# One expert table split ahead of time, eight expert tiles summed per PSUM product, five score tiles handed over late

## The chip, the cores and the metric

The kernel runs on one core of a Trainium2 chip, as one program. The metric is the device time of one execution in microseconds, the median of three runs. The program is written with a tile framework: the code names tiles and operations, and a scheduler at build time decides in which order each engine's queue holds them. At run time every engine (PE, DVE, ACT, POOL, and SP, which only issues DMAs) works through its own queue strictly in order and stops at the first instruction whose inputs or buffers are not ready.

## The reference

One layer: a pair of bidirectional linear-attention mixers on 1024 tokens (with 256 context tokens), then an expert block. The change is about the expert block and what can be prepared for it.

```
def peer(h, wq, k1, k2, u, v):
    q = (tok @ wq).reshape(-1, 8, 2, 128)            # 8 retrieval heads
    s1, s2 = scores of both halves against k1, k2    # 128 keys each
    top 16 of s1, top 16 of s2, top 16 of their 256 sums
    expert = i1 * 128 + i2;  gate = softmax(top_s)   # 128 experts a token
    act = gelu(einsum("pd,ped->pe", xb, u[expert]))
    out = einsum("pe,ped->pd", gate * act, v[expert])
```

`u` and `v` are tables of 16,384 experts (128 tiles of 128) times 1024 columns in float32.

## The kernel before

**Precision.** Large products use float32 operands split into two float16 halves: `split` (L92 to L94) makes the high half on ACT (a scaled copy) and the low half on DVE (scale and subtract). `mm3` (L96 to L101) then does three matmuls for each 128-row step: high x high, high x low, low x high.

**Stages.** (1) `hg_proj`, `hg_scan`, `gla_proj`, `gla_scan`, the "heads", until about 1290 us: input projections, each from a weight slab that `slab` (L175) loads through three buffers `w32`, splits into three buffers `w16`, and feeds to `proj`; there are 65 such slabs. Beside them scans, gates and norms. (2) The merge gates and modulations, to 1500 us. (3) The merge and the output projection, to 1860 us. (4) "Prep", to 2858 us: choosing and routing of tokens (`choosing`, `route`), and one-hot products (`oh`, `pgm`, `gs`) that build `G_d`, the gate of every (token, expert) pair for five of the eight token blocks. (5) The dense stage, to the end.

**Two ways to the experts.** Three token blocks (`GB`) gather their experts' rows: 768 indirect DMAs in all (`row`, issued by POOL at L940), each 128 rows of 4 KB, used by one DVE operation at L919 (dot product with `u`) or L924 (`gacc`, sum with `v`). They have `AHEAD` buffers and run from prep to the end, dosed by `gathers` and `feed`. The other five blocks (`DB`) are done densely: for each of the 128 expert tiles, `u_turn` transposes the `u` tile on PE (`put`), ACT copies it out twice and POOL makes the low half (`uT`, L967); `u_act` multiplies it with the tokens (`ph`, 48 matmuls) and applies GELU (`ac`). `weigh` multiplies `ac` by the gates (`gt`, read from `G_d`) and splits it (`w`). `v_tile` loads the `v` tile (`vn`) and splits it (`v16`). `out_unit` multiplies four tiles' `w` and `v16` into PSUM (`pe`, 24 matmuls for a token block) and DVE adds that to `acc` (L1162).

**Early tiles.** 80 of the 128 tiles' `ac` (the list `early`) are made in prep, one for each `U_US` of the planner's time there, and kept in DRAM (`act_d`), from where the dense stage reads them (`acr`). The other 48 (`live`) are made in the dense stage. It walks through 32 groups of `GR` = 4 experts and, while it prepares a group, does the five `out_unit` of the group before.

**Work between the heads.** `presplit` makes split copies in DRAM of the branch, output and query weights: 40 units, dosed by `meanwhile`, which each projection calls, at `PRE` = 0.25 units a call of full width. Their stores are on ACT's queue (`st_`), the loads on SP's (`ld`).

## Time and profile before

| | us |
|---|---|
| median of three runs (4222.70 to 4229.41) | 4222.92 |
| the profiled execution | 4229.67 |
| its span, first to last instruction | 4228.0 |
| PE busy in it | 3884.8 (92%) |
| DVE busy | 2938.6 (70%) |
| ACT busy | 1430.1 (34%) |
| POOL busy | 1683.9 (40%) |

PE is busy in 92% of the span, but this is an average over stages with different limits; the stages have to be read one by one, with the granted clock of PE (1.00 is its 2.4 GHz level, 0.50 its 1.2 GHz level) and the share of time in which the 16 DMA engines are busy.

### The profile page before, as it was taken

What the parts mean: (1) busy time and instruction counts of PE and PEld (TensorE: products, weight loads), DVE (VectorE), ACT (ScalarE), POOL (GpSimd) and SP (SyncE); (2) the same over time, 40 slices, a digit from 0 to 9 for tenths busy, and PEclk for the clock granted to TensorE, in tenths of its full rate; (3) what the DMA queues carried; (4) which work ended last, traced back from release to release, by engine and by line L of the source; (5) the groups of instructions that cost most, each with busy time, mean ns of one, the idle gap of its engine ahead of it and who ended that gap; (6) DMA issues with size and microseconds to landing.
All of it is one profiled execution on the core that took longest, in us unless ns stands there. A gap on an engine that the chain in (4) does not pass through costs nothing.

```text
span 4228.0 us, 60334 instructions
## 1 busy us (share of the span) xinstructions
PE 3884.8 (92%) x23802; PEld 2350.2 (56%) x23802; DVE 2938.6 (70%) x5132; ACT 1430.1 (34%) x2194; POOL 1683.9 (40%) x1197
## 2 busy tenths in 40 slices
PE   6999999999999999988999989986899989999997
PEld 2665665656655444445776667763445544444453
DVE  5345446242556414379987799977989999889998
ACT  5344444243343202034543334552222222222222
POOL 2011111010011012127655567635766666666663
PEclk9999999999999999999999999987999999999998
DMA  5222122221223583227887778869989999989996
GB/s 189 78 73 85 56 73 79 74 87 46 87 64 115 162 282 107 99 97 242 295 307 249 254 242 298 305 228 319 329 318 336 321 323 325 316 311 325 328 315 232
DMA packets 435306, 884.64 MB, mean 209 GB/s; under 512 B 28511, under 2 KB 245066, under 8 KB 431438
## 3 DMA queue, kind: packets, MB, share of 16 engines
q0 software_dynamic: 110592, 402.70, 27.3%
q1 hardware_dynamic: 202676, 320.19, 22.6%
q10 hardware_dynamic: 121754, 157.89, 10.6%
q8 instruction: 186, 3.05, 0.3%
q14 instruction: 98, 0.80, 0.1%
HBM read 764.80 MB, written 115.88 MB: 208 GB/s over the span
## 4 chain that ended last, share of the span: by engine, by line
PE 47%; DVE 25%; DMA 11%; issue 8%; ACT 6%; POOL 4%; SPq 0%; ACTq 0%; DVEq 0%; POOLq 0%
PE ph L100 5%; DVE row_False L919 5%; PE pe L100 5%; DVE gacc L924 4%; PE pgm L1065 3%; PE pq L100 3%; PE pj_f0h L100 3%; PE pv_g L100 2%; PE pv_h L100 2%; DMA row_False<-in_peer_u_dram,idx 2%; PE pj_f1h L100 2%; PE pj_m L100 2%; DMA vn<-in_peer_v_dram 2%; DMA acr<-act_d 2%; PE pso L100 2%
## 5 line engine op out<-in xcount | busy, mean ns | idle before, releaser
L100 PE MATMUL pe<-v,w 128*128 128x512 f16 x3840 | 883.8, 392 | 138.7 <-DVE acc L1162 104.7
L100 PE MATMUL ph<-hb,uT 128*128 128x256 f16 (+1 forms) x6144 | 892.2, 303 | 14.6 <-POOL uT L967 10.4
L100 PEld LDWEIGHTS <-uT 128*128 128x128 f16 x6144 | 609.4, 99 | 242.5 <-POOL uT L967 13.1
L100 PEld LDWEIGHTS <-w 128*128 128x128 f16 x3840 | 384.0, 100 | 623.0 <-issue 166.4
L940 POOL DMA_INDIRECT row_False<-in_peer_u_dram,idx x384 | 548.9, 1429 | 274.6 <-DVE row_False L919 169.2
L940 POOL DMA_INDIRECT row_True<-in_peer_v_dram,idx x384 | 503.6, 1311 | 264.1 <-DVE gacc L924 173.1
L924 DVE SCALAR_TENSOR_TENSOR gacc<-row_True,dots,gacc 128x1024 f32<-128x1024 f32 x381 | 539.7, 1416 | 39.4 <-DMA row_True<-in_peer_v_dram,idx 35.8
L919 DVE SCALAR_TENSOR_TENSOR row_False<-row_False,h2n 128x1024 f32<-128x1024 f32 x384 | 496.2, 1326 | 67.1 <-DMA row_False<-in_peer_u_dram,idx 66.7
L967 POOL TENSOR_TENSOR uT<-uf,uT 128x512 f16<-128x512 f32 x256 | 380.8, 1499 | 284.0 <-ACT uf L966 282.6
L93 ACT ACTIVATE v<-vn 128x1024 f16<-128x1024 f32 x128 | 135.1, 1055 | 501.9 <-DMA vn<-in_peer_v_dram 386.7
L979 ACT ACTIVATE ac<-ph 128x256 f32<-128x256 f32 (+1 forms) x256 | 110.1, 438 | 371.8 <-PE ph L100 367.1
L1065 PE MATMUL pgm<-oh 128*128 128x128 f16 x1280 | 176.4, 295 | 53.2 <-ACT gs L1066 38.8
L1066 ACT ACTIVATE gs<-pgm 128x512 f32<-128x512 f32 x160 | 171.0, 1069 | 136.6 <-PE pgm L1065 136.6
L94 DVE SCALAR_TENSOR_TENSOR v<-vn,v 128x1024 f16<-128x1024 f32 x128 | 168.2, 1314 | 50.5 <-ACT v L93 50.3
L1162 DVE TENSOR_TENSOR acc<-pe,acc 128x1024 f32<-128x1024 f32 x155 | 188.6, 1217 | 11.8 <-PE pe L100 11.7
L100 PE MATMUL pj_m<-hb,w_m 128*128 128x512 f16 x768 | 187.4, 401 | 2.3 <-DVE lf_g L86 1.6
L1065 PEld LDWEIGHTS <-oh 128*128 128x128 f16 x1280 | 145.7, 117 | 77.0 <-issue 63.5
L100 PE MATMUL pq<-hb,w_wq 128*128 128x512 f16 x768 | 180.0, 387 | 1.0 <-POOL hb L89 0.8
L964 ACT ACTIVATE uT<-put 128x512 f16<-128x512 f32 x256 | 155.0, 605 | 71.0 <-PE put L961 69.4
L89 DVE TENSOR_TENSOR oh<-iota,rTr 128x1024 f16<-128x1024 f16 x160 | 139.1, 879 | 33.9 <-PE pgm L1065 33.8
L100 PEld LDWEIGHTS <-hb 128*128 128x128 f16 x1536 | 150.2, 98 | 17.8 <-issue 0.3
L966 ACT ACTIVATE uf<-put 128x512 f32<-128x512 f32 x256 | 154.4, 603 | 8.9 <-POOL uT L967 8.8
(364 smaller groups left out, 5531.9 us busy)
## 6 DMA issues: line engine op xcount, KB each, us to landing
un<-in_peer_u_dram SPq DMA_DIRECT2D x128, 512.0 KB
vn<-in_peer_v_dram SPq DMA_DIRECT2D x128, 512.0 KB
G_d<-gs ACTq DMA_DIRECT2D x20, 2048.0 KB
gt<-G_d ACTq DMA_DIRECT2D x32, 1280.0 KB
act_d<-ac ACTq DMA_DIRECT2D x80, 320.0 KB
acr<-act_d SPq DMA_DIRECT2D x80, 320.0 KB
mw<-in_ada_w_dram SPq DMA_DIRECT2D x32, 512.0 KB
w_wq<-wq_d SPq DMA_DIRECT2D x32, 512.0 KB
```

The lines of the kernel that those rows point to most:

```text
L89: eng.tensor_tensor(out=out, in0=in0, in1=in1, op=op)
L94: return V.scalar_tensor_tensor(out=lo, in0=src, scalar=float(scale), in1=hi, op0=ALU.mult, op1=ALU.subtract)
L100: PE.matmul(ps, lhsT=a(k), rhs=b(k), start=n == 0, stop=n == last)
L919: V.scalar_tensor_tensor(out=row, in0=row, scalar=1.0, in1=h2n, op0=ALU.mult, op1=ALU.mult, accum_out=dots[:, s:s + 1])
L924: V.scalar_tensor_tensor(out=gacc[n], in0=row, scalar=dots[:, s:s + 1], in1=gacc[n], op0=ALU.mult, op1=ALU.add)
L940: G.indirect_dma_start(out=row, out_offset=None, in_=src[0], in_offset=bass.IndirectOffsetOnAxis(ap=gsel[n][0][:, s:s + 1], axis=0))
L964: S.activation(hi, pv, AF.Copy, scale=SU)
L966: S.activation(uf, pv, AF.Copy, scale=SU)
L967: pace[0] = G.tensor_tensor(out=lo, in0=uf, in1=hi, op=ALU.subtract)
L1065: PE.matmul(pgm[:, t, :], lhsT=oh[:, 0, :, t], rhs=oh[:, j, :, t], start=j == 2, stop=j == 3)
L1066: S.activation(gs[:, :, t0:t0 + TB].rearrange("p i n -> p n i"), pgm, AF.Copy, scale=SA / SG)
L1162: vmark[0] = V.tensor_tensor(out=acc[n], in0=ps, in1=acc[n], op=ALU.add)
```

## The change

Four things. `presplit` also splits all 128 tiles of the table `v` between the projections of the heads and keeps them as float16 pairs in DRAM (`v_d`); `v_tile` then only loads the pair. With that `PRE` is 0.95, its 168 units replace 40, and its stores move from ACT's queue to SP's. Groups have eight experts instead of four, so that an `out_unit` is 48 matmuls into PSUM and one addition; the gates are still read for four (`GH`); `w` and `v16` have 12 buffers each (8 before), and the five units of a group stand in the first half of the next. Score tiles are paced at `U_US` = 7.2 in prep; those that are left then (`rest`, five of them, read off the order of the changed program) are done at the start of the dense stage and stored there, in group 0. The set of early tiles is the first five of each eight instead of a spread. The gathered rows have 5 buffers instead of 6, `feed` has other weights, and the SBUF area reserved for descriptors of DMAs that POOL issues is set to 4096 bytes a partition.

```diff
-GR = 4
+GR = 8
+GH = 4
+NBUF = 12
-U_US = 6.2
+U_US = 7.2
-AHEAD = 6
-PRE = 0.25
+AHEAD = 5
+PRE = 0.95
-    early = [e for e in range(NKEY) if e * 5 % 8 < 5]
+    early = [e for e in range(NKEY) if e % 8 < 5]
...
+            def rows(src, dst, sc, nm):
+                w32 = wi.tile([P, D], F32, name=f"w32_{nm}", tag="w32", bufs=3)
+                ld(out=w32, in_=src)
+                w16 = ws.tile([P, 2, D], F16, name=f"w16_{nm}", tag="w16", bufs=3)
+                split(w32, w16[:, 0], w16[:, 1], sc)
+                ld(out=dst, in_=w16)
...
+            more = slabs()
+            for e in range(NKEY):
+                rows(v_r[e], v_d[e], SV, f"v{e}")
                 yield
+                if e % 3 == 2:
+                    next(more, None)
+                    yield
+            yield from more
...
-        while pend is not None:
-            early_tile()
...
-        tt(V, v3, v3, gt4[:, :, e % GR, :], ALU.mult)
-        w16 = pd.tile([P, 2, TD], F16, name=f"w16_{e}", tag="w16", bufs=2 * GR)
+        tt(V, v3, v3, gt4[:, :, e % GH, :], ALU.mult)
+        w16 = pd.tile([P, 2, TD], F16, name=f"w16_{e}", tag="w16", bufs=NBUF)
...
-        vn = pd.tile([P, D], F32, name=f"vn{e}", tag="vn", bufs=2)
-        ld(out=vn, in_=v_r[e])
-        v16 = pd.tile([P, 2, D], F16, name=f"v16_{e}", tag="v16", bufs=2 * GR)
-        vmark[0] = split(vn, v16[:, 0], v16[:, 1], SV)
+        v16 = pd.tile([P, 2, D], F16, name=f"v16_{e}", tag="v16", bufs=NBUF)
+        ld(out=v16, in_=v_d[e])
...
+    rest = [pend, *es] if pend is not None else []
+    todo = []
+    for j in range(GR):
+        todo += [j] * (j in live) + rest[2 * j:2 * j + 2]
+    todo += rest[2 * GR:] + [e for e in live if e >= GR]
...
-    work = lambda e: 2.1 if e in early else 9.5
+    work = lambda e: (7.5, 7.5, 7.5, 7.5, 1.0, 2.5, 2.5, 2.5)[e % GR]
...
+                if g == 0:
+                    for r in rest[2 * j:2 * j + 2] if j < GR - 1 else rest[2 * j:]:
+                        st_(out=act_d[early.index(r)], in_=next_act(r))
...
-                    for n in DB[j * NU // GR:(j + 1) * NU // GR]:
+                    for n in DB[min(j * NU // GH, NU):(j + 1) * NU // GH]:
                         out_unit(g - 1, n, *prev)
...
-    nc = _bacc.Bacc("TRN2", target_bir_lowering=False, num_devices=1)
+    nc = _bacc.Bacc("TRN2", target_bir_lowering=False, num_devices=1, dynamic_dma_scratch_size=4096)
```

**In the heads** SP's queue holds the loads of the weight slabs (`w_f1h`, `w_qh`, `w_gh`: slabs of a head's projections; `w_pb`: a branch weight for `presplit`). Before, between the slabs `w_f1h` and `w_qh`:

```order
L179 DMA w_f0h_999<-in_w_in_dram 128x8x128
L179 DMA w_f1h_1083<-in_w_in_dram 128x8x128
L179 DMA w_pb_1140<-in_w_branch_hgrn_dram 128x8x128
L179 DMA w_qh_1173<-in_w_in_dram 128x8x128
L179 DMA w_gh_1335<-in_w_in_dram 128x8x128
```

In the changed program, at the same two slabs (`w_v` is a tile of the table `v`, `v_d` and `br_d` are where split copies go):

```order
L182 DMA w_f1h_1144<-in_w_in_dram 128x8x128
L326 DMA br_d<-w_pb_1107 128x2048
L318 DMA w_v_1175<-in_peer_v_dram 128x1024
L321 DMA v_d<-w_v_1139 128x2048
L318 DMA w_v_1207<-in_peer_v_dram 128x1024
L182 DMA w_pb_1239<-in_w_branch_hgrn_dram 128x8x128
L321 DMA v_d<-w_v_1177 128x2048
L182 DMA w_qh_1246<-in_w_in_dram 128x8x128
```

One transfer stood between the two slabs, now six do, three of them stores that wait for a split.

**At the hand-over** from prep to the dense stage ACT's queue holds the last copies of the one-hot products (`gs`), the store of `G_d` and the reads of the gates (`gt`). Before:

```order
L1066 ACTIVATE gs_3_24807<-pgm_124_24902 128x4x128
L1068 DMA G_d<-gs_3_24807 128x4096
L1180 DMA gt_24949<-G_d 128x20x128
L93 ACTIVATE v_0_24955<-vn_24953 128x1024
L93 ACTIVATE v_1_25041<-vn_25039 128x1024
L1180 DMA gt_25193<-G_d 128x20x128
L1140 CAST w_0_24959<-acr_24951 128x640
```

In the changed program:

```order
L1082 ACTIVATE gs_3_24998<-pgm_124_25264 128x4x128
L980 ACTIVATE uT_25308<-put_1_25318 128x512
L1084 DMA G_d<-gs_3_24998 128x4096
L982 ACTIVATE uf_1_25324<-put_1_25318 128x512
L995 ACTIVATE ac_25327<-ph_120_25328 128x256
L995 ACTIVATE ac_25327<-ph_120_25354 128x384
L980 ACTIVATE uT_25383<-put_0_25384 128x512
L1223 DMA act_d<-ac_25327 128x640
L1212 DMA gt_25290<-G_d 128x20x128
```

Score tiles (`put`, `ph`; here tiles 120 and 121) now stand between the store of `G_d` and the reads of it, and four more follow.

**In the dense stage** DVE's queue holds the additions to `acc` (the number behind `pe` is the token block), the gathered rows' operations, the splits of `v` and of `w`. Before, over four additions:

```order
L1162 TENSOR_TENSOR acc_24926<-pe_6_28448,acc_24926 128x1024
L94 SCALAR_TENSOR_TENSOR v_44_28515<-vn_28513,v_44_28515 128x1024
L1162 TENSOR_TENSOR acc_24927<-pe_7_28474,acc_24927 128x1024
L924 SCALAR_TENSOR_TENSOR gacc_14435<-row_48_True,dots_24271,gacc_14435 128x1024
L1141 TENSOR_TENSOR w_44_28519<-acr_28511,w_44_28519 128x640
L924 SCALAR_TENSOR_TENSOR gacc_14435<-row_49_True,dots_24271,gacc_14435 128x1024
L94 SCALAR_TENSOR_TENSOR v_45_28555<-vn_28553,v_45_28555 128x1024
L924 SCALAR_TENSOR_TENSOR gacc_14435<-row_50_True,dots_24271,gacc_14435 128x1024
L1162 TENSOR_TENSOR acc_24923<-pe_2_28525,acc_24923 128x1024
```

In the changed program, from one addition to the next but one:

```order
L1174 TENSOR_TENSOR acc_25286<-pe_3_31206,acc_25286 128x1024
L935 SCALAR_TENSOR_TENSOR row_34_False,dots_30546<-row_34_False,h2n_30544 128x1024
L935 SCALAR_TENSOR_TENSOR row_35_False,dots_30546<-row_35_False,h2n_30544 128x1024
L935 SCALAR_TENSOR_TENSOR row_36_False,dots_30546<-row_36_False,h2n_30544 128x1024
L935 SCALAR_TENSOR_TENSOR row_37_False,dots_30546<-row_37_False,h2n_30544 128x1024
L935 SCALAR_TENSOR_TENSOR row_38_False,dots_30546<-row_38_False,h2n_30544 128x1024
L935 SCALAR_TENSOR_TENSOR row_39_False,dots_30546<-row_39_False,h2n_30544 128x1024
L91 TENSOR_TENSOR acr_31469<-acr_31469,gt_31467 128x640
L1174 TENSOR_TENSOR acc_25287<-pe_5_31282,acc_25287 128x1024
```

The splits of `v` are gone from DVE, and six or seven rows' operations stand between two additions where one to six stood.

## Rows read from the trace of the kernel before

**Rows 1.** The page: busy time of each engine.
```profile
PE 3884.8 (92%) x23802; PEld 2350.2 (56%) x23802; DVE 2938.6 (70%) x5132; ACT 1430.1 (34%) x2194; POOL 1683.9 (40%) x1197
```
**Rows 2.** Stages: window, length, busy PE, PEld, DVE, ACT, POOL, clock, DMA share, GB/s.
```profile
80.00:1290.00 1210.00, 1177.13 (x8071) 750.22 (x8069) 562.58 (x940) 475.97 (x664) 161.55 (x87) 0.99 0.24 72
1290.00:1500.00 210.00, 192.68 (x1060) 100.88 (x1058) 106.88 (x163) 48.10 (x74) 12.38 (x6) 0.95 0.54 170
1860.00:2858.00 998.00, 913.29 (x6518) 680.21 (x6516) 869.94 (x1976) 449.46 (x733) 587.66 (x444) 0.97 0.74 261
2878.00:4170.00 1292.00, 1178.03 (x6238) 623.76 (x6239) 1173.71 (x1289) 338.13 (x525) 842.57 (x585) 0.95 0.92 321
```
**Rows 3.** Timeline of PE in the dense stage: start, length, what; idle before, releaser.
```profile
3312.39 13.24 PE L100 MATMUL pe<-v,w 128*128 128x512 f16 x48 [4.89 <-DVE acc L1162]
3325.47 1.04 PE L961 MATMUL put<-ident,un 128*128 128x128 f32 x8
3326.35 6.68 PE L100 MATMUL ph<-hb,uT 128*128 128x256 f16 x48
3332.87 20.93 PE L100 MATMUL pe<-v,w 128*128 128x512 f16 x96
...
3394.63 5.75 PE L100 MATMUL pe<-v,w 128*128 128x512 f16 x14 [5.32 <-DVE acc L1162]
```
**Rows 4.** Groups by line, 2878 to 4170 us: busy, mean ns, idle before, releasers.
```profile
L100 PE MATMUL pe<-v,w 128*128 128x512 f16 x3686 | 847.4, 391 | 132.3 <-DVE acc L1162 98.3 <-ACT w L1140 27.7 <-DVE w L1141 5.5
...
L924 DVE SCALAR_TENSOR_TENSOR gacc<-row_True,dots,gacc 128x1024 f32<-128x1024 f32 x243 | 334.7, 1377 | 4.3 <-DMA row_True<-in_peer_v_dram,idx 1.7
L919 DVE SCALAR_TENSOR_TENSOR row_False<-row_False,h2n 128x1024 f32<-128x1024 f32 x253 | 319.5, 1300 | 22.5 <-DMA row_False<-in_peer_u_dram,idx 22.2
L1162 DVE TENSOR_TENSOR acc<-pe,acc 128x1024 f32<-128x1024 f32 x148 | 180.1, 1217 | 10.4 <-PE pe L100 10.3
L94 DVE SCALAR_TENSOR_TENSOR v<-vn,v 128x1024 f16<-128x1024 f32 x127 | 167.0, 1315 | 30.1 <-ACT v L93 30.0
...
L940 POOL DMA_INDIRECT row_True<-in_peer_v_dram,idx x250 | 334.1, 1336 | 212.7 <-DVE gacc L924 165.8 <-issue 27.7 <-DVE row_False L919 9.6
```
**Rows 5.** Two windows of 42 us in the dense stage, columns as in rows 2.
```profile
3554.00:3596.00 42.00, 34.22 (x171) 17.27 (x171) 38.22 (x52) 10.79 (x16) 27.11 (x20) 0.92 1.00 351
3596.00:3638.00 42.00, 42.00 (x239) 23.45 (x238) 33.23 (x44) 11.11 (x19) 25.68 (x17) 1.00 0.81 274
```
**Rows 6.** Who waited for the stores to wq_d: us, times.
```profile
  ACT w_m L93: 23.7, 5
  ACT w_gg L93: 8.4, 3
```
**Rows 7.** Groups by line, 1860 to 2858 us, PE.
```profile
L100 PE MATMUL ph<-hb,uT 128*128 128x256 f16 (+1 forms) x3936 | 582.9, 304 | 13.7 <-POOL uT L967 10.4 <-ACT ac L979 3.2
...
L961 PE MATMUL put<-ident,un 128*128 128x128 f32 x680 | 93.4, 277 | 6.2 <-ACT uf L966 6.2
```
**Rows 8.** Timeline of PE at the hand-over, 2824 to 2890 us.
```profile
2831.84 1.10 PE L1065 MATMUL pgm<-oh 128*128 128x128 f16 x8 [1.14 <-ACT gs L1066]
2877.97 1.46 PE L100 MATMUL pe<-v,w 128*128 128x512 f16 x3 [20.40 <-ACT w L1140]
```
**Rows 9.** The page's DMA parts: a queue's packets and MB; sizes of transfers.
```profile
q0 software_dynamic: 110592, 402.70, 27.3%
...
vn<-in_peer_v_dram SPq DMA_DIRECT2D x128, 512.0 KB
...
gt<-G_d ACTq DMA_DIRECT2D x32, 1280.0 KB
```
**Rows 10.** Timeline of PE, 4100 to 4228 us: its last product.
```profile
4199.66 13.34 PE L100 MATMUL pe<-v,w 128*128 128x512 f16 x48 [5.30 <-DVE acc L1162]
```
**Rows 11.** The chain that ended last, pieces in order of time: start, us, what.
```profile
2909.12 8.17 DMA row_False<-in_peer_u_dram,idx
...
3582.45 7.14 DMA row_False<-in_peer_u_dram,idx
```

More of the change, by code (lines that the diff above doesn't have):

```diff
@@ L130, in tile_layer @@
     wo_d = dram.tile([KC, P, 2, D], F16, name="wo_d")
+    v_d = dram.tile([NKEY, P, 2, D], F16, name="v_d")
     u_r = peer_u[0].rearrange("(e p) d -> e p d", p=NKEY)
@@ L311, in presplit, with slabs @@
         def presplit():
-            for j in range(KC):
-                for bi, w in ((0, w_br_gla), (1, w_br_hg)):
-                    st_(out=br_d[bi * KC + j], in_=slab(w[0], j * P, f"pb{bi}{j}", SW))
-                    yield
-            for k in range(KC):
-                w32 = wi.tile([P, D], F32, name=f"wo32_{k}", tag="w32", bufs=3)
-                ld(out=w32, in_=w_out[k * P:(k + 1) * P, :])
-                w16 = ws.tile([P, 2, D], F16, name=f"wo16_{k}", tag="w16", bufs=3)
-                split(w32, w16[:, 0], w16[:, 1], SW)
-                st_(out=wo_d[k], in_=w16)
+            def rows(src, dst, sc, nm):
[4 more added lines that the diff above has]
+                ld(out=dst, in_=w16)
+            def slabs():
+                for j in range(KC):
+                    for bi, w in ((0, w_br_gla), (1, w_br_hg)):
+                        ld(out=br_d[bi * KC + j], in_=slab(w[0], j * P, f"pb{bi}{j}", SW))
+                        yield
+                for k in range(KC):
+                    rows(w_out[k * P:(k + 1) * P, :], wo_d[k], SW, f"wo{k}")
+                    yield
+                for j in range(16):
+                    ld(out=wq_d[j], in_=slab(peer_wq[0], j * P, f"pq{j}", SWQ))
+                    yield
+            more = slabs()
+            for e in range(NKEY):
+                rows(v_r[e], v_d[e], SV, f"v{e}")
                 yield
-            for j in range(16):
-                st_(out=wq_d[j], in_=slab(peer_wq[0], j * P, f"pq{j}", SWQ))
-                yield
+                if e % 3 == 2:
+                    next(more, None)
+                    yield
+            yield from more
         ahead = presplit()
@@ L1166, in tile_layer, with next_act @@
     live = [e for e in range(NKEY) if e not in early]
-    uT = u_turn(live[0], u_load(live[0]))
-    li = 0
-    work = lambda e: 2.1 if e in early else 9.5
+    rest = [pend, *es] if pend is not None else []
[3 more added lines that the diff above has]
+    todo += rest[2 * GR:] + [e for e in live if e >= GR]
+    if not rest:
+        uT = u_turn(todo[0], u_load(todo[0]))
+    ahead_ = iter(todo[1:])
+    def next_act(e):
+        nonlocal uT
+        en = next(ahead_, None)
+        uTn = u_turn(en, u_load(en)) if en is not None else None
+        ac = u_act(e, uT)
+        uT = uTn
+        return ac
+    work = lambda e: (7.5, 7.5, 7.5, 7.5, 1.0, 2.5, 2.5, 2.5)[e % GR]
     left = [sum(map(work, range(NKEY))), 256 * len(GB) - done[0]]
@@ L1178, in tile_layer @@
         if g < NG:
-            gt4 = pd.tile([P, TD // NB, GR, NB], F32, name=f"gt{g}", tag="gt4", bufs=2)
-            st_(out=gt4, in_=G_d[:, :, g * GR:(g + 1) * GR, :].rearrange("b i j n -> i b j n"))
             cur = ([None] * GR, [None] * GR)
@@ L1183, in tile_layer @@
                 e = g * GR + j
+                if j % GH == 0:
+                    gt4 = pd.tile([P, TD // NB, GH, NB], F32, name=f"gt{e}", tag="gt4", bufs=2)
+                    st_(out=gt4, in_=G_d[:, :, e:e + GH, :].rearrange("b i j n -> i b j n"))
                 if e in early:
@@ L1187, in tile_layer @@
                 else:
[L1188 to L1193 removed]
+                    ac = next_act(e)
                 cur[1][j] = v_tile(e)
@@ L1210, in tile_layer @@
             for n in range(NT):
-                x1s[n] = pd.tile([P, D], F32, name=f"x1_{n}", tag="v16", bufs=2 * GR)
+                x1s[n] = pd.tile([P, D], F32, name=f"x1_{n}", tag="v16", bufs=NBUF)
                 ld(out=x1s[n], in_=x1_d[n * P:(n + 1) * P, :])
```

6 lines of the change are left out of this document (removed).

## The prediction

> **What bounds the kernel now.** I read the engines' shares first, then the table by stage, and in each stage the idle time in front of PE and what ended it. PE is busy for 3884.8 of 4228.0 us [rows 1], but the 343 idle us lie in few places. The heads (80 to 1290) are PE's: 1177.1 of 1210 us, only 32.9 idle, while DVE is busy for 562.6, ACT for 476.0 and the DMA engines for 0.24 of the stretch [rows 2]. So there is room beside PE for other work, as long as nothing makes PE's next weights late. Prep (1860 to 2858) has PE at 913 and DVE at 870 of 998 [rows 2]. Then PE stands for 20.4 us [rows 8]. The dense stage is the one to look at: PE 1178.0, DVE 1173.7 of 1292 us and the DMA share 0.92 at 321 GB/s. Three resources are above 0.9 there, so taking one away shows the next.
>
> Of the three, DVE is the one that PE waits for. Eight experts take 3394.63 - 3312.39 = 82.2 us, and at the start of each such piece PE stands for about 5 us with `acc` as releaser [rows 3]; over the stage `acc` released 98.3 of the 132.3 idle us in front of the `pe` products [rows 4]. `acc` is short (1.22 us), but stands in DVE's queue behind row operations and splits. After the stall 48 `pe` matmuls take 13.24 us, where 96 together take 20.93, that is 10.46 for 48 [rows 3], and the granted clock of such a window is 0.92 against 1.00 without the stall [rows 5]: the stall costs some 3 us more than itself. With no stall and full clock, eight experts are 240 `pe` x 0.218 (20.93/96) = 52.3, three live tiles at 0.88 + 6.52 = 7.40 from start to start [rows 3], 22.2: **74.5 us**.
>
> **The heads.** Each of the 128 tiles of `v` adds a load, an ACT copy, a DVE split and a store. The split costs 1.315 us of DVE [rows 4], 128 x 1.315 = 168 us, and ACT's copy no more than that; 562.6 + 168 and 476 + 168 stay far below 1210. The DMAs are 512 KB in and 512 KB out, 134 MB, which is 111 GB/s over 1210 us on top of 72; the stage at 1860 has moved 261 [rows 2]. The dose of 0.95 units a call ends the 170 units by the end of the merge gates (the calls of full width there and before are some 180); that stage stands at 170 GB/s [rows 2], so the same rate on top leaves it at 281, under the dense stage's 321. In total this is free. What is not free is order: the added units share SP's queue and the three buffers `w32` and `w16` with the weight slabs, and a store on SP waits for its split while the next slab's load is queued behind it. Of slab, split and store at work beside the heads the trace has 40 units. All of PE's idle time there is 32.9 us, 0.82 a unit, and that includes causes of their own; so 128 units cost from 0 to 128 x 0.82 = 105 us. I take **+25**, a quarter: part of what went before was that the stores sat in ACT's queue (23.7 us in 5 waits, 4.7 each, 8.4 in 3 [rows 6]) and ACT made the very splits that PE waited for; these waits go. An added unit also lacks room in no total.
>
> **Prep and hand-over.** 80 early tiles become 75 there, a difference of about 4.75 with the one that is in work at the end. One costs 582.9/82 = 7.11 for its `ph` and 93.4/85 = 1.10 for its `put` (3936 and 680 instructions, 48 and 8 a tile [rows 7]), 8.2 us; 4.75 x 8.2 = **-39**. The one-hot products (`pgm`) that end prep have no early tile left beside them now: the row shown is 1.1 us of work behind 1.1 us of idle time, and there are some 13 like it up to 2858, 15 us [rows 8]. With the slower pace tiles last to the end, **-15**. The gap of 20.4 us at the hand-over, in which `G_d` is stored and read back [rows 8], does not become shorter, but tiles 120 and 121 stand in it: its gain is in the next sum, since they would otherwise lie in front.
>
> **The dense stage.** From DVE go 128 splits of `v` (167.0 us) and half of the additions (180.1/2 = 90) [rows 4]; by the 15.7 pieces of eight experts in 1292 us, 16.4 of 74.7 us. DVE has 58 to 65 us of work per 74.5 and PE's wait for `acc` loses its cause: six or seven rows between two additions are at most 7 x 1.38 = 9.6 us, under the 10.5 of a unit's 48 matmuls. ACT loses the copies too. PE would fall to 74.5.
>
> Then DMA is next. In one piece of eight experts the changed kernel moves 32.5 rows of 402.70/768 = 0.524 MB [rows 9], 17.0; `v`, the same 512 KB a tile in halves, 4.2; three `un` 1.6; five `acr` of 128 x 640 x 4 bytes 1.6; two `gt` of 1280 KB 2.6: **27.1 MB**. The densest window has share 1.00 and 351 GB/s, and its neighbour 0.81 at 274 [rows 5], both 338 to 351 per unit of share. At 351 the 27.1 MB take 77.1 us, at 321, the mean of the stage before, 84.3. Both are over 74.5, so the transfers bind, by little. I take 345, **78.5 us**, nearer to the full window, as PE and DVE no longer stop at a fixed place. The Trainium skill, in "HBM Reference", section "Specifications (TRN2)", says that a core streaming alone measures about 425 GB/s; by that figure the piece would take an estimated 63.7 us and DMA would bind nothing. No row here shows more than 351, at a share of 1.00, so the sum goes by the row.
>
> Before, 2858 to the end was 1370 us. After: group 0 has three live tiles and five `rest` tiles, 8 x 7.4 = 59, no units, and the hand-over in it, whose first gates are needed 20 us in; from 55 (all hidden) to 83 (a whole piece, 59 + 20 and more), I take 75. Fifteen groups at 78.5 are 1177.5 (74.5 to 84.3 each). Then five last units, 52.3, and 15 from the end of PE's last product (4199.66 + 13.34 [rows 10]) to 4228, as now. Sum 1319.8, that is **-50**.
>
> Smaller edits. `acr` of the rest tiles is written and read back as before. The area for descriptors is 4096 bytes and no row shows how much is used; POOL issues a row in 1336 ns and has 27.7 us of idle time without a releaser in 250 issues [rows 4], so from the rows its cost is between 0 and what one row less in flight would cost, which is the second rival. I take 0.
>
> **Sum.** 4228 + 25 - 39 - 15 - 50 = 4149 on the profiled span. The median of the runs is 4222.9, 5.1 below that span (the profiled execution was at 4229.7, 6.8 above the median): **4144**.
>
> **The rivals.** *DMA does not bind.* If the share can stay at 1.00 with more than 351 GB/s, or the row queue's transfers merely stretch into idle room, PE is the limit: 74.5 a group, 55 for group 0. That is 15 x 4.0 + 20 = 80 less, **4064**. For it: PE and the engines are still stopped in every piece now, so nobody has seen the DMAs pushed. Against: the full windows occur already [rows 5]. The Trainium skill's section named above leads to this rival.
>
> *Five rows in flight are too few.* Rows are issued when a buffer comes free: five in issue (1.34 us), landing and use (1.35). In the 52 us of five units 26 rows stand in DVE's queue in front of the additions, one per 2.01 us. Five buffers keep up if landing takes at most 5 x 2.01 - 1.4 - 1.35 = 7.3 us. The chain has two row transfers of 7.14 and 8.17 us [rows 11], on both sides of that. At 8.17 a row comes every 2.18 us, 26 of them take 56.8, 4.5 more than the units: PE waits for `acc` again, by 15 x 4.5 = 67 us, **4211**. For it: waits for rows are 22.2 and 1.7 us with six buffers [rows 4], and a fuller DMA lands later.
>
> *The heads pay (the slower side).* The place is SP's queue in the heads, where between two slabs now stand six transfers, three of them stores which wait for a split, in a ring of three buffers. If the load of a slab is held until the store before it is released and PE is through its own work by then, each of the 65 slabs costs its lateness. In the trace a store held ACT for 4.7 us in the longer waits [rows 6]; the row of eight waits gives 4.0 in the mean, and `slab` has a lead of several us. Total gain elsewhere is 104, so it decides from 104/65 = 1.6 us a slab. At 2.8, the middle of 1.6 and 4.0, it is 182 instead of 25, **4301**. For it: PE has only 33 us of slack there. Against: PE's part of a slab is 1177/65 = 18 us, long against six transfers of 0.5 to 1 MB.
>
> **How the numbers follow.** Forecast 4144 with 0.50, DMA not binding 4064 with 0.20, five rows too few 4211 with 0.15, the heads' loss 4301 with 0.12, anything else 0.03. The measurement can tell about 0.2% from no change, so faster is below 4214.5 and slower above 4231.4. Faster: the forecast nearly whole, the first rival, and two thirds of the second, 0.79; same 0.07 (the rest of the second, and of the forecast if heads come to 105); slower 0.14. The range leaves out the slower rival and the far ends: 4055 (10 below the first rival, for heads at 15 instead of 25) to 4215 (the second).
>
> **What would show it.** Heads: PE idle between 80 and 1290 about 58 us instead of 33, the stage ending 25 later; if it grows by over 130 the third rival holds, and the trace must then name weights (`w_...`) as releaser of PE. Hand-over: `ph` products between the last `pgm` and the first `pe`. Dense: no 5 us stalls for `acc` at the head of a piece, clock 1.00, a period of 78.5 us for eight experts at a DMA share of 0.97 or more and about 345 GB/s, with PE's waits moved to `v`, `acr` or `uT` data that a DMA releases. If the period is 74.5 at a higher rate, the first rival; if DVE waits long for rows and PE for `acc` with the share below 0.95, the second. Wrong altogether would be a landing time of `row` transfers over 9 us.

## The result and the profile after

The changed kernel takes 4273.72 us (median; 4267.74 to 4277.66) against 4223.81 for the kernel before: a ratio of 1.0114, 95% interval 1.0097 to 1.0132. It is slower by 1.1%; 4144 was forecast, and the range ended at 4215. The profiled execution has a span of 4265.9 us, 37.9 more than before.

The table by stage of the changed kernel (window, length, busy PE, PEld, DVE, ACT, POOL, clock, DMA share, GB/s), to be read beside [rows 2]:

```profile
80.00:1290.00 1210.00, 1139.90 (x7634) 720.72 (x7633) 672.96 (x969) 560.84 (x741) 161.72 (x85) 0.97 0.50 163
...
1860.00:2858.00 998.00, 910.47 (x6354) 666.73 (x6352) 882.80 (x2135) 445.50 (x721) 552.27 (x425) 0.97 0.71 250
...
2878.00:4170.00 1292.00, 1173.85 (x6243) 626.55 (x6241) 973.78 (x1088) 225.93 (x415) 782.54 (x600) 0.95 0.92 328
```

In the heads PE loses 37 us of busy time and its granted clock falls from 0.99 to 0.97. In the dense stage DVE has 200 us less to do (257 were forecast), and PE is no busier for it: 1173.9 of 1292 us, where it was 1178.0. So the relief of DVE did not reach PE.

Four marks on PE's timeline cut the span: the first query product (`pq`), the last one-hot product (`pgm`, its start and length), and the first `pe` of the second and of the last group of eight. In the changed kernel:

```profile
1687.93 0.38 PE L102 MATMUL pq<-hb,w_wq 128*128 128x512 f16 x1
...
2858.50 1.10 PE L1081 MATMUL pgm<-oh 128*128 128x128 f16 x8
...
3048.92 4.70 PE L102 MATMUL pe<-v,w 128*128 128x512 f16 x21
...
4202.56 4.70 PE L102 MATMUL pe<-v,w 128*128 128x512 f16 x21
```

In the kernel before (whose groups have four experts; the last two marks have as many `pe` matmuls, 240, ahead of and behind them as in the changed kernel):

```profile
1621.88 0.38 PE L100 MATMUL pq<-hb,w_wq 128*128 128x512 f16 x1
...
2856.47 1.10 PE L1065 MATMUL pgm<-oh 128*128 128x128 f16 x8 [1.11 <-ACT gs L1066]
...
2976.25 4.04 PE L100 MATMUL pe<-v,w 128*128 128x512 f16 x10 [2.11 <-DVE acc L1162]
...
4142.73 3.57 PE L100 MATMUL pe<-v,w 128*128 128x512 f16 x8 [9.11 <-DVE acc L1162]
```

| | before | after | difference | forecast |
|---|---|---|---|---|
| to the first `pq` (heads, merge) | 1621.9 | 1687.9 | +66 | +25 |
| to the end of the last `pgm` (prep) | 1235.7 | 1171.7 | -64 | -54 |
| from there to the end (dense) | 1370.4 | 1406.3 | +36 | -50 |
| sum | 4228.0 | 4265.9 | +38 | -79 |

Between the last two marks lie 14 periods of eight experts (3360 `pe` matmuls in both traces): (4142.73 - 2976.25)/14 = 83.3 us before, (4202.56 - 3048.92)/14 = 82.4 after. "The period" below is this mean.

**The dense stage.** What is late there is told by the waits from 2840 us to the end, in the changed kernel (who waited for what: us in total, times, longest):

```profile
DVE row_False L935 <- DMA row_False<-in_peer_u_dram,idx: 121.8, 62, 11.9
...
DVE gacc L940 <- DMA row_True<-in_peer_v_dram,idx: 62.3, 70, 4.1
...
PE ph L102 <- POOL uT L983: 61.0, 21, 7.1
...
PE pe L102 <- ACT w L1154: 40.2, 11, 10.6
...
PE pe L102 <- DVE acc L1174: 8.6, 8, 3.1
```

PE's wait for `acc` is nearly gone (98.3 us in [rows 4]), as forecast. But DVE now waits 184 us for gathered rows (24 in [rows 4]), and PE waits for `uT` and `w` instead. The way from the rows to PE can be seen on POOL's timeline:

```profile
3447.11 1.36 POOL L956 DMA_INDIRECT row_True<-in_peer_v_dram,idx  x1
3448.49 2.27 POOL L983 TENSOR_TENSOR uT<-uf,uT 128x512 f16<-128x512 f32 x2
3452.92 1.88 POOL L956 DMA_INDIRECT row_True<-in_peer_v_dram,idx  x1 [2.16 <-DVE gacc L940]
3455.11 0.94 POOL L956 DMA_INDIRECT row_True<-in_peer_v_dram,idx  x1 [0.30 <-issue]
3456.06 2.27 POOL L983 TENSOR_TENSOR uT<-uf,uT 128x512 f16<-128x512 f32 x2
```

POOL's queue holds row issues and `uT` of the live tiles in one order. At 3452.92 the issue had waited 2.16 us until DVE released a buffer, and two `uT` stood behind it. DVE, in its own order, waits for rows and has `acr` and `w` behind them. So a ring of five buffers that comes round too slowly would stop both engines that feed PE; the runs on the ring below test this.

**The heads.** The longest case is on ACT's timeline:

```profile
93.76 1.06 ACT L95 ACTIVATE w_pb<-w_pb 128x1024 f16<-128x1024 f32 x1 [10.02 <-DMA v_d<-w_v]
94.72 0.58 ACT L587 ACTIVATE at_f0h<-pj_f0h 128x512 f32<-128x512 f32 x1
```

and on PE's:

```profile
95.35 5.26 PE L102 MATMUL pj_f1h<-hb,w_f1h 128*128 128x512 f16 x12 [4.30 <-ACT at_f0h L587]
```

ACT stood for 10.02 us before a copy into a `w16` buffer whose last owner's store to `v_d` had not landed. The copy of a projection out of PSUM (`at_f0h`) stood behind, and PE waited 4.30 us for its PSUM buffer. The five largest rows of ACT's waits for such stores from 80 to 1290 us are 141 us:

```profile
ACT w_v L95 <- DMA v_d<-w_v: 69.1, 25, 6.4
...
ACT w_pb L95 <- DMA v_d<-w_v: 21.3, 4, 10.0
...
ACT w_qh L95 <- DMA v_d<-w_v: 18.5, 4, 6.0
...
ACT w_pq L95 <- DMA v_d<-w_v: 16.3, 7, 6.4
...
ACT w_gh L95 <- DMA v_d<-w_v: 15.4, 4, 4.1
```

All rows for the stores of split copies together are 222 us. Such waits are not new: for its 40 units the kernel before has 87 us of them in the same window. What is new is that ACT has less time left to wait in. The time that it waited for PE in this window fell from 518 to 216 us; for one of its copies, before and after:

```profile
ACT at_f0h L571 <- PE pj_f0h L100: 82.2, 18, 14.5
```

```profile
ACT at_f0h L587 <- PE pj_f0h L102: 21.3, 11, 3.4
```

In its place stand the added waits for stores (135 us) and for loads (20 us before, 74 after) and 85 us more of ACT's own work. Up to the first `pq` PE's waits that ACT ended grew from 17 to 55 us, and those that DVE ended from 31 to 47.

**The hand-over.** DVE's timeline after the last `pgm`:

```profile
2888.69 1.56 DVE L91 TENSOR_TENSOR acr<-acr,gt 128x640 f32<-128x640 f32 x2 [30.85 <-DMA gt<-G_d]
```

DVE stands 30.85 us for the first gates, with row operations behind it. From the last `pgm` to the second group's first `pe` are 3048.92 - 2859.6 = 189 us, where the forecast has 75 + 78.5 = 153.5. PE is idle for 43 of them, and its mean granted clock there is 0.88.

### The profile page after: what moved, and what is told of

It is laid out like the page before. It is cut to its first block, busy times and chain, and to the rows that moved or that the text cites. A ratio compares the mean times of both kernels' runs of the same rounds, so it can differ in the third digit from the quotient of the medians.

```text
span 4265.9 us, 60698 instructions
## 1 busy us (share of the span) xinstructions
PE 3904.9 (92%) x23802; PEld 2356.2 (55%) x23802; DVE 2894.8 (68%) x5052; ACT 1439.7 (34%) x2198; POOL 1604.2 (38%) x1197
## 4 chain that ended last, share of the span: by engine, by line
PE 39%; DVE 17%; DMA 15%; issue 14%; POOL 8%; ACT 7%; SPq 0%; ACTq 0%; POOLq 0%; DVEq 0%
PE ph L102 6%; DMA row_False<-in_peer_u_dram,idx 4%; DMA row_True<-in_peer_v_dram,idx 3%; PE pgm L1081 3%; POOL row_True L956 3%; POOL row_False L956 3%; DVE row_False L935 3%; PE pe L102 3%; PE pq L102 2%; PE pj_f1h L102 2%; DMA v_d<-w_v 2%; PE pv_g L102 2%; PE pso L102 2%; PE pj_qh L102 2%; ACT gs L1082 2%
## 5 line engine op out<-in xcount | busy, mean ns | idle before, releaser
L102 PE MATMUL ph<-hb,uT 128*128 128x256 f16 (+1 forms) x6144 | 923.3, 308 | 80.3 <-POOL uT L983 77.7
L102 PE MATMUL pe<-v,w 128*128 128x512 f16 x3840 | 850.6, 384 | 52.7 <-ACT w L1154 40.2
L935 DVE SCALAR_TENSOR_TENSOR row_False<-row_False,h2n 128x1024 f32<-128x1024 f32 x384 | 512.4, 1362 | 164.6 <-DMA row_False<-in_peer_u_dram,idx 163.6
L956 POOL DMA_INDIRECT row_False<-in_peer_u_dram,idx x384 | 497.0, 1294 | 305.5 <-DVE row_False L935 209.4
L940 DVE SCALAR_TENSOR_TENSOR gacc<-row_True,dots,gacc 128x1024 f32<-128x1024 f32 x381 | 524.2, 1376 | 78.6 <-DMA row_True<-in_peer_v_dram,idx 74.7
L983 POOL TENSOR_TENSOR uT<-uf,uT 128x512 f16<-128x512 f32 x256 | 350.4, 1381 | 245.1 <-ACT uf L982 243.5
L96 DVE SCALAR_TENSOR_TENSOR w_v<-w_v,w_v 128x1024 f16<-128x1024 f32 x128 | 167.3, 1308 | 196.3 <-ACT w_v L95 196.1
L1154 ACT CAST w<-acr 128x640 f16<-128x640 f32 x80 | 56.5, 723 | 643.4 <-PE pe L102 358.3
L1081 PE MATMUL pgm<-oh 128*128 128x128 f16 x1280 | 176.4, 295 | 38.8 <-ACT gs L1082 28.1
L95 ACT ACTIVATE w_v<-w_v 128x1024 f16<-128x1024 f32 x128 | 134.9, 1055 | 171.6 <-DMA v_d<-w_v 72.8
L977 PE MATMUL put<-ident,un 128*128 128x128 f32 x1024 | 141.4, 279 | 15.4 <-ACT uf L982 15.3
```

The costliest lines, as they stand in the source:

```text
L95: S.activation(hi, src, AF.Copy, scale=float(scale))
L96: return V.scalar_tensor_tensor(out=lo, in0=src, scalar=float(scale), in1=hi, op0=ALU.mult, op1=ALU.subtract)
L102: PE.matmul(ps, lhsT=a(k), rhs=b(k), start=n == 0, stop=n == last)
L935: V.scalar_tensor_tensor(out=row, in0=row, scalar=1.0, in1=h2n, op0=ALU.mult, op1=ALU.mult, accum_out=dots[:, s:s + 1])
L940: V.scalar_tensor_tensor(out=gacc[n], in0=row, scalar=dots[:, s:s + 1], in1=gacc[n], op0=ALU.mult, op1=ALU.add)
L956: G.indirect_dma_start(out=row, out_offset=None, in_=src[0], in_offset=bass.IndirectOffsetOnAxis(ap=gsel[n][0][:, s:s + 1], axis=0))
```

## The experiments

**The heads: two more buffers.**

```diff
-                w16 = ws.tile([P, 2, D], F16, name=f"w16_{nm}", tag="w16", bufs=3)
+                w16 = ws.tile([P, 2, D], F16, name=f"w16_{nm}", tag="w16", bufs=5)
```

(at all places of the tag `w16` with three buffers, `slab` among them)

> The changed kernel, with five buffers w16 instead of three in the heads, for weight slabs and split v tiles alike; nothing else. Theory A: the heads grew by 66 us (first query product 1621.9 to 1687.9 us) because a w16 buffer is only free when its store, queued on SP, has landed; ACT stands at the next copy until then, and PE waits for ACT's other copies out of PSUM. Then two more buffers give back at least 40 of the 66 us: total at or below 4234, ACT's waits for v_d stores near zero. Rival: it is the load itself (168 us more DVE work, 135 more ACT work, DMA traffic beside the weights) that delays PE. Then less than 15 us come back: 4258 or more.

Measured: 4232.96 us, ratio to before 1.0015 (1.0003 to 1.0027). The first `pq` starts here:

```profile
1656.97 0.38 PE L102 MATMUL pq<-hb,w_wq 128*128 128x512 f16 x1
```

31 of the 66 us come back by the first `pq`, and 41 in all. The total is where theory A put it, but two of its signs failed: fewer than 40 of the 66 us came back, and ACT's waits for stores to `v_d` (80 to 1290 us, all rows) fell only from 173 to 145 us, not to nearly none. PE's idle time up to the first `pq` fell from 104.9 to 77.9 us (53.3 before the change). So the ring is a cause, but half of the loss is left, and most of the waits that were to explain it are still there. A sixth buffer was to tell whether the rest is ring or load:

> The changed kernel with six buffers w16 in the heads (five gave the first query product at 1657.0 us instead of 1687.9; before it was at 1621.9). Theory A (the ring): 5 to 15 us earlier again, first query product at 1642 to 1652, total 4218 to 4230. Rival (what is left is the load of the added ACT and DVE work itself): within 4 us of 1657, total 4228 to 4240.

Measured: 4246.97 us, first `pq` at 1674.93: worse than five, which neither side expected. Theory A, as put, falls: ACT's waits for loads of `v` tiles between 80 and 1550 us, 63.2 us with five buffers, were 96.5 with six. The scheduler orders the queues anew for each ring; that this is the reason is not shown. Then the stores were put back on ACT's queue:

```diff
-                ld(out=dst, in_=w16)
+                st_(out=dst, in_=w16)
```

(and the stores to `br_d` and `wq_d` likewise)

> The changed kernel with five buffers w16 in the heads, and the stores of the split copies on ACT's queue again, as before the change, instead of SP's. Theory D (loads of slabs and v tiles are late because SP's queue holds stores that wait for a split): loads come earlier, first query product 10 to 25 us earlier than 1657. Rival: ACT's queue, which makes the copies and empties PSUM, now holds store issues that wait for DVE's split: the first query product 10 us or more later than 1657.

Measured: 4299.68 us, first `pq` at 1717.45, 60 us later than with the stores on SP. The rival held: with five buffers that part of the change, which moved the stores to SP, is worth having.

**Parts of the change alone or undone.** (Groups of eight and the new weights of `feed` were not run by themselves.)

> The kernel before, with the split of v in the heads alone: presplit, its stores on SP and its dose as in the changed kernel, v loaded as a pair in the dense stage. Groups of four, six row buffers and the old hand-over stay. Theory A/B: heads +66 as in the changed kernel, but the dense stage gains, since DVE loses 10.5 of 74.7 us per eight experts and no row buffer is lost: a period of 76 to 79 instead of 82.2, 50 to 90 us less, total 4200 to 4240. Rival (the DMA engines bind any arrangement at 92 to 95%): the period stays at 81 to 83, total 4275 to 4295.

Measured: 4278.39 us (1.0125; 1.0108 to 1.0142); period (4194.40 - 3035.44)/14 = 82.8. The heads cost the same here (first `pq` at 1684.5), and relieving DVE of the split brings the dense stage nothing: time and period are in the ranges of the rival. The waits from 2912 to 4210 us:

```profile
DVE acr L89 <- DMA acr<-act_d: 103.4, 39, 7.4
...
PE pe L100 <- DVE acc L1174: 92.4, 32, 7.1
```

DVE's work falls to 1026.8 us in these 1298, but it waits 103 us for `acr` transfers where it waited 13.6 before, and `acc`, behind them in the queue, is as late as ever (92.4 against 98.3 in [rows 4]). So the sum of DVE's work was not what made the stall at the head of a group. Whether the rival's cause holds, that the DMA engines bind (their share is 0.90 here), this run does not tell, for the trace names another place too: SP's queue, which issues the `acr` loads, stood 518 us of the 14 periods until `put` on PE freed a `un` buffer, and 152 us before. That the order of these queues makes the stall (PE, SP, DVE, and PE again) is read from the waits, not tested.

Next, the left-over score tiles made in prep:

```diff
+        while pend is not None:
+            early_tile()
     prep_st.close()
```

> The changed kernel, but the score tiles left at the end of prep are made there, as before, and none in group 0. Theory C: in the changed kernel DVE stands 31 us for the first gates with row operations behind them, POOL stands at row issues, and the live tiles' uT behind these, so group 0 takes 110 us from the last one-hot product to the first product of group 1. Made ahead of it, the five tiles cost 41 us and group 0 35 to 60: 10 to 32 us less, total 4242 to 4264. Rival: the five tiles are hidden where they stand, and come on top: 15 to 40 us more, 4289 to 4314.

Measured: 4291.23 us, 17 more than the changed kernel: theory C missed, and the rival is right. By the 17 us, not quite half of the five tiles' 41 us is hidden where they stand in the changed kernel, so that part of the change is a gain.

**The ring of rows.** One more row buffer needs 4 KB a partition, which one `v16` buffer gives; so its control has 11 of these.

```diff
-AHEAD = 5
+AHEAD = 6
-        v16 = pd.tile([P, 2, D], F16, name=f"v16_{e}", tag="v16", bufs=NBUF)
+        v16 = pd.tile([P, 2, D], F16, name=f"v16_{e}", tag="v16", bufs=NBUF - 1)
```

> The changed kernel with 11 instead of 12 buffers v16: the control for the next run, which needs the room. v loads wait one tile longer for PE on SP's queue. All theories: within 10 us of the changed kernel, 4264 to 4284, dense stage 1396 to 1416, mean period from group 1 on 82 to 83.

Measured: 4269.08 us, period (4204.19 - 3045.24)/14 = 82.8.

> The changed kernel with 11 buffers v16 and six row buffers instead of five. Theory B (five rows in flight are too few: DVE waits for rows, POOL stands at an issue that waits for DVE, live tiles' uT behind it): the mean period falls from 82.4 to 78 to 80, DVE's waits for rows (183 us in the dense stage) by half or more, total 30 to 60 us less than the control, 4215 to 4245. Rival (DMA engines bind, a sixth row only lands later): landing grows from 6.0 us by about a fifth, the period moves by less than 1 us, total within 12 us of the control.

Measured: 4218.26 us (0.9982; 0.9972 to 0.9991), period (4161.15 - 3044.21)/14 = 79.8: 51 us less than the control, for one buffer. DVE's waits for rows from 2840 us on fell from 185 to 99 us, a little less than by half.

> The changed kernel with 10 buffers v16 and seven row buffers. Theory B: the gain over the control goes on but smaller, 5 to 15 us below the run with six, DVE's waits for rows nearly gone. Rival: no difference to the run with six or with five; landing grows by another sixth.

Measured: 4188.35 us (0.9919; 0.989 to 0.9948), period (4124.39 - 3024.17)/14 = 78.6. That is 30 below six, more than expected; 17 of them are in the 14 periods, and most of the others ahead of the second group. The same two waits of DVE, and PE's for `uT`, with five rows (the control), from 2840 us on:

```profile
DVE row_False L935 <- DMA row_False<-in_peer_u_dram,idx: 119.6, 60, 10.0
...
DVE gacc L940 <- DMA row_True<-in_peer_v_dram,idx: 65.5, 70, 5.2
...
PE ph L102 <- POOL uT L983: 54.0, 19, 5.4
```

and with seven:

```profile
DVE row_False L935 <- DMA row_False<-in_peer_u_dram,idx: 50.2, 38, 10.3
...
PE ph L102 <- POOL uT L983: 16.5, 9, 3.4
...
DVE gacc L940 <- DMA row_True<-in_peer_v_dram,idx: 7.1, 13, 1.5
```

The rival wanted longer landings. The median from issue to landing is, in the changed kernel (five) and with seven:

```profile
row_False<-in_peer_u_dram,idx POOLq DMA_INDIRECT x384, 6.4
row_True<-in_peer_v_dram,idx POOLq DMA_INDIRECT x384, 7.0
```

```profile
row_False<-in_peer_u_dram,idx POOLq DMA_INDIRECT x384, 6.9
row_True<-in_peer_v_dram,idx POOLq DMA_INDIRECT x384, 7.2
```

That is 0.5 us at most, where the rival asked for more than a third in two steps. Over the 14 periods the DMA engines went from 328 GB/s at a share of 0.92 in the control to 347 at 0.95. So with five rows they had room, and the ring was the bound.

**The ring in the kernel before.** `AHEAD = 5` there, and `AHEAD = 9` with the smaller descriptor area:

> The kernel before with five row buffers instead of six, nothing else. Theory B: DVE's queue is the bound there and a late row makes it later still: dense stage 20 to 45 us longer, total 4245 to 4270. Rival (a buffer is not what rows wait for; DVE has 91% of the stage and rows land before it is free): within 10 us of the kernel before.

Measured: 4250.93 us (1.0061; 1.0039 to 1.0082), 24 us for the sixth buffer.

> The kernel before with an area for descriptors of 4096 bytes, as in the changed kernel, and nine row buffers in the room that this frees. Theory B': before, DVE is the bound and six buffers nearly do; three more give 0 to 15 us, total 4210 to 4227, and the smaller area costs nothing. Rival 1 (the area for descriptors holds back row issues): POOL's idle time without a releaser grows, 10 us or more slower. Rival 2 (rows in flight were the bound before, too): 30 to 60 us faster.

Measured: 4213.19 us (0.9973; 0.9963 to 0.9983), 12 us faster. So six nearly do before the change, and the smaller area, changed together with the ring, has no cost that shows. The step from five rows to six is worth 24 us in the kernel before and 51 in the changed one.

**Do the DMA engines bind?** First in the changed kernel, and then with the ring mended, only the first tiles of `v` are loaded (12 and 10) and used again, so that the products with `v` are of wrong tiles:

```diff
-        v16 = pd.tile([P, 2, D], F16, name=f"v16_{e}", tag="v16", bufs=NBUF)
...
+        if e >= NBUF:
+            return few[e % NBUF]
...
```

> The changed kernel, but only the first twelve v tiles are loaded in the dense stage and used again for all others: 4.2 of 27.1 MB of transfers per eight experts are left out, and SP's queue is rid of loads that wait for PE. Theory B (the ring of five rows, in which a transfer's landing and DVE's in-order use follow each other): the period falls by less than 2 us from 80 to 82, total above 4240. Rival (DMA engines bind): rows land sooner and the period falls to 75 to 77, 75 to 100 us less, total 4175 to 4200, with a DMA share under 0.88.

Measured: 4255.1 us, of which some 36 are the longer end; period (4158.60 - 3051.34)/14 = 79.1. That is between both expectations. Rows land in 6.1 and 6.2 us instead of 6.4 and 7.0, so lighter transfers shorten the ring's round too; DVE still waits 106 us for rows in the 14 periods (149 in the changed kernel).

> The run best, but only the first ten v tiles are loaded and used again for all others: 4.2 of 27.1 MB per eight experts left out (the end is some 36 us longer, as x1 then has two buffers). Theory E (with seven rows in flight the DMA engines bind at a period of 78.5 us and 344 GB/s): the period falls to 75 to 76 us, at a share near 0.85. Rival (PE waits for DVE's order and not for transfers): it stays at 77.5 or more.

Measured: one execution of 4136.62 us; period (4035.56 - 2984.05)/14 = 75.1. From 3000 to 4030 us the window of this run, then that of its parent (`best`, below):

```profile
3000.00:4030.00 1030.00, 1019.61 (x5597) 550.13 (x5596) 863.82 (x938) 192.92 (x356) 684.70 (x530) 1.00 0.88 305
```

```profile
3000.00:4030.00 1030.00, 995.09 (x5373) 530.12 (x5374) 834.40 (x922) 187.12 (x344) 650.94 (x507) 0.98 0.95 348
```

Without 4.2 MB a group PE is busy 99% at a clock of 1.00, and the period is PE's own 74.5 but for 0.6. With them it is 78.7 at 348 GB/s. That is what theory E expected, at the price the forecast had put on the transfers (78.5 us, 345 GB/s). But the run takes away two things at once: the bytes, and the loads of `v` from SP's queue. In `best` these stand 508 us of the 14 periods until PE frees a `v16` buffer, and loads of `acr` are queued among them, for which DVE waits here from 2840 us on:

```profile
DVE acr L91 <- DMA acr<-act_d: 76.5, 28, 12.0
```

Without them DVE waits 47 us for `acr` in the 14 periods, although an `acr` load takes 7.3 us from issue to landing in both runs; a `un` load lands in 5.2 instead of 7.5 us. So that the transfers bind once enough rows are in flight is likely, but no run here keeps the bytes and changes only the order of SP's queue, or the reverse.

**Both remedies.** Five `w16`, seven rows, ten `v16`:

> The changed kernel with five buffers w16 in the heads, seven row buffers and ten buffers v16: the two remedies together. If heads and dense stage are separate causes, they add up: 4273.7 - 40.7 - 85.4 = about 4148, 4135 to 4162, faster than both kernels. If one cause feeds the other (the heads' delay, or a dense stage that only waits elsewhere), 4165 or more.

Measured: 4156.64 us (0.9841; 0.9824 to 0.9859): 1.6% faster than the kernel before. The two causes add up but for 9 us, within the expectation; the period is (4092.79 - 2991.28)/14 = 78.7, as with seven rows alone.

**What is left of the heads.** On top of `best`, a fourth buffer `w32`:

> The run best with four instead of three buffers w32 for the loads of slabs and v tiles. Theory A2 (ACT's waits for loads, 63 us for v tiles and 28 for w_m in the heads, are the ring of loads): the first query product comes at 1635 to 1648 instead of 1654.8, total 4138 to 4150. Rival (the load of the added ACT and DVE work, or the order in which ACT's queue holds the copies): 1650 to 1660 or later, total 4150 to 4170.

Measured: 4150.57 us (0.9817; 0.98 to 0.9834), not to be told from `best`; first `pq` at 1660.51. The rival held: ACT's waits for loads from 80 to 1290 us fell from 113 to 40 us, and PE was no earlier. Then the copies that `presplit` makes of `v` and `w_out` on another engine:

```diff
-                split(w32, w16[:, 0], w16[:, 1], sc)
+                tsc(V, w16[:, 0], w32, sc, ALU.mult)
+                V.scalar_tensor_tensor(out=w16[:, 1], in0=w32, scalar=sc, in1=w16[:, 0], op0=ALU.mult, op1=ALU.subtract)
```

(with `G` for the first `V` in the second run)

> The run best, with the high half of the split v and w_out tiles made by DVE instead of ACT. Theory A3 (what is left of the heads' cost is ACT, which stands for loads, stores and buffers of the added tiles while PE waits for its copies out of PSUM): the first query product comes at 1625 to 1640 instead of 1654.8, total 4125 to 4143. Rival (DVE is as much in PE's chain, or the transfers themselves are the cost): 1650 or later, total 4150 or more.

Measured: 4158.92 us, first `pq` at 1663.65.

> The run best, with the high half of the split v and w_out tiles made by POOL instead of ACT. Theory A3: first query product at 1622 to 1642, total 4120 to 4145, since POOL has 164 us of work in the 1210 of the heads. Rival: POOL's own part of the scans (kc, ke, lf) stands behind the split tiles then, or POOL and DVE hinder each other: 1655 or later, total 4155 or more.

Measured: 4323.11 us, first `pq` at 1831.17. Theory A3 falls: whichever engine makes the copies takes over the waits (in the heads and gates, 80 to 1550 us, DVE now waits 67.0 us for stores to `v_d`, POOL 150.0), and PE is as late or later. With DVE making the copies, ACT again waits 397 us for PE from 80 to 1290 us (229 in `best`), so giving ACT its spare time back does not by itself bring PE forward. What the remaining 33 us of the heads are (1654.8 against 1621.9) stays open; 21 of them are idle time of PE, the others more busy time for the same products.

**What is left of the hand-over.** On top of `best`:

```diff
-                if g == 0:
-                    for r in rest[2 * j:2 * j + 2] if j < GR - 1 else rest[2 * j:]:
-                        st_(out=act_d[early.index(r)], in_=next_act(r))
...
+                if e == 0:
+                    for r in rest:
+                        st_(out=act_d[early.index(r)], in_=next_act(r))
+                        gathers(G_E)
```

(ahead of `weigh`)

> The run best, with the five left-over score tiles and 17 row uses all ahead of the first multiplication with the gates, so that DVE does not stand for the gates with row operations behind it. Theory C: DVE's wait of 34 us for the first gates goes, PE's holes of 11.5 us and after it too; from the last one-hot product to the first full unit of group 0 106 us become 80 to 92: total 4132 to 4145. Rival (the hand-over's 41 us of tiles and the 22 of live tiles must be made anyway, the rest is the transfers at 365 GB/s): within 6 us of best, 4150 to 4163.

Measured: 4156.8 us. DVE's wait for the gates fell from 33.9 to 13.0 us, and nothing came of it: the second group starts later (3003.4 us against 2991.3), the periods after it are shorter (78.0 against 78.7). The rival's range held, and DVE's wait was not what made the hand-over long. A stage that the transfers bind would give just this picture; no run here shows that for the hand-over by itself.

## Why the prediction was wrong, point by point

The step that failed in the dense stage is the one from DVE to the DMA engines: the forecast let them be the next bound at 78.5 us a period and left the ring of five rows, the second rival, out of the sum; the ring held the period at 82.4. The heads (+25) and group 0 (75) were mis-sized beside it.

- **Heads, +25: mis-sized, +66.** The bounds (0 to 105) held the value; taking a quarter of the way was the error. The reason for it was that waits for stores leave ACT when their issue does; ACT's waits for the landing of stores grew instead, from 87 to 222 us, as 168 units came at nearly four times the pace of the 40. "An added unit also lacks room in no total" was so for busy time; but busy time, waits for stores and waits for loads together left ACT 216 us in which it waited for PE, where it had had 518. PE then waited for ACT's copies out of PSUM. Of the 66 us, 52 are idle time of PE up to the first `pq` (104.9 against 53.3), and 14 more busy time for the same products, at a mean granted clock of 0.97 instead of 0.98. 16 of the idle us are at one place after the heads, the products `pmd` of the modulations (0.8 before), which wait for DVE; why DVE is late there is open, as are 33 of the 66 us in all. The third rival named the place, the ring of three, but charged a weight's lateness to each slab; that price, +182, did not come, and the trace names no weight's transfer as releaser of PE. (The six transfers between two slabs are 512 KB each, not "0.5 to 1 MB".)
- **Prep, -54: near, -64.** The one-hot products' waits fell by 14 us (53.2 to 38.8; 15 were forecast). The tiles gave 51 us (`ph` 582.9 to 539.0, `put` 93.4 to 86.3) instead of 39: the forecast divided by the 82 tiles that stand there before the change, but took the difference from 80.
- **DVE's relief.** "PE's wait for `acc` loses its cause" was right (98.3 us to 8.6), and that PE is then free of DVE was not. The run with the split of `v` alone shows that DVE's 91% was not the cause even of the stall: 147 us less work over a stretch as long (1173.7 and 1026.8 us), and 0.5 us off the period.
- **Five rows too few: the rival that came, at 0.15.** Its price was 67 us in 15 pieces; two more buffers give 4.2 us a period against the control, 14 x 4.2 = 59, and 81 with the start and the end. Its working named DVE and PE's wait for `acc`. In its place the wait went through POOL (`uT` behind row issues) and DVE (`w` behind rows). That the price came near is in part luck, for its round trip was too short: it had issue, landing and use, 1.4 + 6.4 + 1.35 = 9.2 us with the median landing, but at 454 rows in the 14 periods, one in 2.54 us, five buffers come round in 12.7. The difference, an estimate of 3.5 us, is the time in which a landed row waits its turn on DVE and a free buffer its turn on POOL. Without those two waits 7.3 us of landing looked affordable.
- **DMA price, 78.5 us a period: met, but not the bound of the changed kernel.** It shows as soon as seven rows are in flight (78.6), and without 4.2 MB a period, and their loads in SP's queue, the period is 75.1. So the first rival, 74.5 with all the bytes, did not come in any run. The Trainium skill's figure for one core streaming alone ("HBM Reference", section "Specifications (TRN2)", about 425 GB/s) is in no window read here; the most is 365 GB/s over 40 us at the hand-over, and 350 over 1030 us at a share of 0.95, with seven rows.
- **Group 0, 75: mis-sized, about 110.** 189 us to the second group against 153.5 (and 176 still in `best`). Gates 30 us late were not in the bound of 83, but with 21 us of that wait gone the second group came no earlier. The longest stops of PE there are 10.6 us for `w` and 10.0 for `uf` from ACT and 7.1 for `uT` from POOL. Which cause lies behind them stays open.
- **The sum.** Heads +41 on the forecast, prep -10, group 0 +36, 14 periods x 3.9 = +55, the end -4: 4149 + 118 = 4267, the measured span but for 1.

## What to carry to other kernels

A ring of transfers is sized by its whole round: issue, landing, use, and the time that a landed buffer and a free buffer each wait in an in-order queue; taking a buffer away to make room for something else is priced by that, and what matters is who else stands in the queues of issuer and user. Taking work off an engine at 91% brought nothing here, as the next thing in its queue was waited for instead: look at what stands in the queue, not at its sum alone. Work that is moved under a busy engine is hidden only as long as the engine's helper keeps time to spare: add up its busy time and its waits in the shared rings, and see how long it still waits for the busy engine.

## What the runs showed of the hardware

Where DVE and POOL work at the same time, some DVE operations take several times as long. `w` of a live tile took 0.86 us on average before (41.1 us for 48), and 1.72 in the changed kernel:

```profile
L1141 DVE TENSOR_TENSOR w<-ac,w 128x640 f16<-128x640 f32 x48 | 41.1, 857 | 32.9 <-ACT w L1140 32.6
```

```profile
L1155 DVE TENSOR_TENSOR w<-ac,w 128x640 f16<-128x640 f32 x47 | 80.9, 1721 | 36.6 <-ACT w L1154 36.6
```

and on DVE's timeline two of them stand at the very times of POOL's `uT` shown above:

```profile
3448.43 3.02 DVE L1155 TENSOR_TENSOR w<-ac,w 128x640 f16<-128x640 f32 x1 [0.79 <-ACT w L1154]
...
3455.50 3.53 DVE L1155 TENSOR_TENSOR w<-ac,w 128x640 f16<-128x640 f32 x1 [0.79 <-ACT w L1154]
```

The first is 2.2 us longer than a `w` that stands alone (0.82), and POOL's two `uT` beside it take 2.27. Both end 0.7 us after the second `uT` does (3451.45 after 3450.76, 3459.03 after 3458.33), as if they had waited for it. The Trainium skill ("SBUF — State Buffer", section "SBUF: two separate sides") says that a DVE operation with two inputs in SBUF and a GpSimd operation that reads SBUF exclude each other, and the later one waits. The trace agrees in that one of the two waits; here it is DVE, although both `w` are recorded as starting before the `uT` (by 0.06 and 0.56 us), so which one came first the records do not show. In the sum of the prediction these 40 us of DVE over the stage (80.9 against 41.1) were missing.

The same scaled copy to float16 of 128 x 1024 takes 808 ns on DVE and 3013 on POOL:

```profile
L86 DVE TENSOR_SCALAR w_v<-w_v 128x1024 f16<-128x1024 f32 x126 | 101.7, 808 | 136.9 <-DMA v_d<-w_v 67.0 <-DMA w_v<-in_peer_v_dram 20.5 <-DMA br_d<-w_pb 13.0
```

```profile
L86 POOL TENSOR_SCALAR w_v<-w_v 128x1024 f16<-128x1024 f32 x118 | 355.3, 3013 | 565.2 <-DMA v_d<-w_v 150.0 <-DMA w_v<-in_peer_v_dram 114.4 <-DMA br_d<-w_pb 69.1
```
